# Delta rule rewritten: a shared inverse, a written order on three engines, output tiles as a stage of their own

## The chip, the cores and the metric

The kernel runs on one core of one Trainium2 chip. A core has five engines that run at the same time, each with its own queue that it works off in order: TensorE (PE; its weight loads appear as PEld), VectorE (DVE), ScalarE (ACT), GpSimd (POOL) and SyncE (SP, which here only issues DMA transfers). They wait for each other by semaphores. Matmuls read SBUF and write PSUM, which has 8 banks. The metric is the device time of one execution in microseconds (us).

## The reference

One step of a two-layer encoder over 2048 prompt tokens and 32 sample tokens (2080 rows of 1024), in float32. Layer A is a gated delta rule with 8 heads of 128; layer B is windowed attention.

```python
proj = x @ w_in                                   # q, k, v, z (1024 each), a, b
q, k, v = silu(short causal conv(proj)); q, k l2-normalised
beta = sigmoid(b);  g = -exp(a_log) * softplus(a + dt_bias);  gcum = cumsum(g) in a chunk
tmat = I + strict_lower(beta * k k^T * decay)     # decay = exp(gcum_i - gcum_j)
u, w = tmat^-1 (beta v),  tmat^-1 (beta k exp(gcum))
for chunk:                                        # S is a 128x128 state per head
    v_new = u - w S
    o = (q exp(gcum)) S + (q k^T * decay) v_new
    S = S exp(g_last) + (k exp(g_last - gcum))^T v_new
h = layer_norm(ALPHA * x + (rms_norm(o) * silu(z)) @ w_out)
y = layer_norm(ALPHA * h + attention(h))          # layer B: rotary q, shared k/v, sinks, gate
```

## The kernel before

**P1** (from 0 to about 700 us) projects the inputs, slab by slab of 128 columns over 5 token blocks of 416. Every product is made of three matmuls (high times high, high times low, low times high), so one block is 24 matmuls on PE (`project`). `P1.z` makes the gate z; blocks 0 to 2 come first, blocks 3 and 4 later, beside the delta rule. Results go to DRAM and come back by DMA.

**Delta** works through 17 chunks: 16 of 128 tokens and the 32 of the sample. Per chunk and in halves q of four heads: `decays` makes the decay matrix E (DVE and ACT), `lower` multiplies k k^T by it (tile npr), gathers the 32x32 diagonal blocks (nb) and lays them out with a DVE transpose (tile L, L414). `chain` inverts these blocks for all heads at once: 31 pairs of short instructions (L421 makes tm from L and Tt, L423 subtracts it from Tt), each waiting for the one before. It runs on GpSimd, for the second chunk alone on VectorE. `spread` turns the result Tt around (tcp, ucp) into t32 and u32; `invert` completes the 128x128 inverse u by five rounds of small matmuls (bps). `turn_k`, `turn_v`, `inside` make kd, vn and at, and fade k and q. `errors` (ks, rho, vp, vs) and `advance` (op, o, sp, Sp) are the recurrence over chunks; `scale` and `emit` normalise o, turn it (otr), multiply it by z and store it (s_g).

`run` is the loop. In iteration i chunk i is finished, chunk i+1 is inverted and chunk i+2 is begun. The order on PE is the order in which the code is written (`manual_schedule`); DVE, ACT and the DMA queues are ordered by a scheduler at build time.

**Filler**: between the steps `fill(us)` lets PE do other work of so many us: first z of blocks 3 and 4 (`P1.z`), then the output tiles **O1**. An output tile is 128 tokens: g is loaded (L727), split into high and low parts (g_hi on ACT L737, g_lo on GpSimd L738), multiplied by w_out in two halves of 24 matmuls (po, L751 to L753), added to x and normalised on DVE (L756 to L775), turned on PE (tr, L797) into hT and stored. g and hT share one buffer. After the last chunk the rest of the 17 tiles runs without the delta rule, with two gate blocks of P2 among them.

**P2** and **Attention** follow: the projections of layer B (PE bound) and the attention.

Of the kernel before, what the change touches and what calls it, by code (L numbers as in the profile page):

```python
# [43 lines left out]
def split_weights(nc, pool, src, sub):  # L44

    raw = pool.tile([128, KC, 128], F32, tag="w_raw", name="w_raw", bufs=1)
    hi = pool.tile([128, KC, 128], F32R, tag="w_hi", name="w_hi")
    lo = pool.tile([128, KC, 128], F32R, tag="w_lo", name="w_lo")
    nc.sync.dma_start(raw[:], src)
    nc.scalar.copy(hi[:], raw[:])  # L50
    sub.tensor_tensor(out=lo[:], in0=raw[:], in1=hi[:], op=ALU.subtract)  # L51
    return hi, lo

# [34 lines left out]
class P1:  # L88
# [3 lines left out]
    def __init__(self, tc, left, right, I, O, T, G):  # L92
# [4 lines left out]
        self.ppl = new_pool(tc, left, "p1_psl", 3, PSUM, side="left")  # L97
# [3 lines left out]
        self.ppr = new_pool(tc, right, "p1_psr", 3, PSUM, side="right")  # L101
# [32 lines left out]
    def ps(self):  # L134
        self.turn += 1
        return (self.ppl, self.ppr)[self.turn % 2].tile([128, 512], F32, tag="ps", name="ps")
# [75 lines left out]
    def z(self, blocks, pool, tags, ps, sub):  # L212
        nc = self.nc
        for h in range(8):
            w = split_weights(nc, self.wp, self.I["w_in"][24 + h], sub)
            for b in blocks:
# [7 lines left out]
                nc.sync.dma_start(self.T["z"][h, :, b * TB:(b + 1) * TB], z[:])  # L224

# [84 lines left out]
def rsqrt_newton(nc, pool, x, n, w, tag):  # L310
    V = nc.vector
    y = pool.tile([128, w], F32, tag=tag + "_y", name=tag + "_y")
# [3 lines left out]
    V.tensor_scalar(out=y[:n].bitcast(I32), in0=y[:n].bitcast(I32), scalar1=-1, scalar2=0x5F3759DF,  # L316
                    op0=ALU.mult, op1=ALU.add)
    for _ in range(3):
        V.scalar_tensor_tensor(out=t[:n], in0=x[:n], scalar=-0.5, in1=y[:n], op0=ALU.mult, op1=ALU.mult)
        V.tensor_tensor(out=t[:n], in0=t[:n], in1=y[:n], op=ALU.mult)  # L320
        V.scalar_tensor_tensor(out=y[:n], in0=t[:n], scalar=1.5, in1=y[:n], op0=ALU.add, op1=ALU.mult)
    return y
# [7 lines left out]
class Delta:  # L330


    def __init__(self, tc, es, I, O, T, G):
# [9 lines left out]
        self.pc = new_pool(tc, es, "d_pc", 2, PSUM, side=R)  # L343
        self.nm = one.tile([128, 128], F32, tag="nm", name="nm")
        nc.scalar.dma_start(self.nm[:], I["nm"])
        self.tinit = one.tile([128, 32, 8], F32, tag="tinit", name="tinit")
        nc.scalar.dma_start(self.tinit[:], I["tinit"])
        self.f = {}
        for k in ("t32", "u32", "m1"):
            self.f[k] = one.tile([128, 8, 64], F32, tag=k, name=k)  # L350
            nc.vector.memset(self.f[k][:], 0.0)
        self.u = one.tile([128, 8, 128], F32, tag="u", name="u")
        nc.vector.memset(self.u[:], 0.0)
        self.S = one.tile([128, 8, 128], F32, tag="Sp", name="Sp")
        nc.vector.memset(self.S[:], 0.0)
# [5 lines left out]
    def load(self, ch, name):  # L361
        nc, T, n = self.nc, self.T, ch.n
        ts = slice(ch.t0, ch.t0 + n)
        pool, bufs = (self.sml, 2) if name == "v" else (self.four, 4)
        tiles = []
        for q in range(2):
            hs = slice(q * 4, q * 4 + 4)
            t = pool.tile([128, 4, 128], F32, tag=name, name=name, bufs=bufs)
# [5 lines left out]
        setattr(ch, name, tiles)  # L374

    def decays(self, ch):
        nc, V, G = self.nc, self.nc.vector, self.G
        n, ti = ch.n, ch.ti
        ch.E = []
        for q in range(2):  # L380
# [3 lines left out]
            for j in range(4):  # L384
                nc.scalar.activation(E[:n, j, :n], E[:n, j, :n], AF.Exp, bias=G["ngc"][:n, ti, q * 4 + j:q * 4 + j + 1])
            V.tensor_tensor(out=E[:n, :, :n], in0=E[:n, :, :n], in1=self.bc(G["cc"][:n, ti, q * 4:q * 4 + 4], n, n),
                            op=ALU.mult)
            ch.E.append(E)

    def lower(self, ch):  # L390
# [4 lines left out]
        ch.nb = nb = self.sml.tile([128, 8, 32], F32, tag="nb", name="nb")  # L395
        for q in range(2):
# [5 lines left out]
            if q == 1:  # L402
                for b in range(n // 32):
                    bs = slice(32 * b, 32 * b + 32)
                    nc.scalar.copy(nb[bs], ch.npr[bs, :, bs])
            yield "kk"

    def chain(self, ch, P):

        nc, V = self.nc, self.nc.vector  # L410
        n = ch.n
        sml = self.sml
        L = sml.tile([128, 32, 32], F32, tag="L", name="L")
        V.transpose(L[:n], ch.nb[:n].rearrange("q p i -> q i p").unsqueeze(2).to_broadcast([n, 32, 4, 8]))  # L414
        Tt = self.two.tile([128, 32, 8], F32, tag="Tt", name="Tt")
        tm = sml.tile([128, 32, 8], F32, tag="tm", name="tm")
        nc.scalar.copy(Tt[:n], self.tinit[:n])
        for j in range(31):
            i0, w = j + 1, j // 4 + 1
            sh = [n, 31 - j, w]  # L420
            P.tensor_tensor(out=tm[:n, i0:, :w], in0=L[:n, i0:, j:j + 1].to_broadcast(sh),  # L421
                            in1=Tt[:n, j:j + 1, :w].to_broadcast(sh), op=ALU.mult)
            P.tensor_tensor(out=Tt[:n, i0:, :w], in0=Tt[:n, i0:, :w], in1=tm[:n, i0:, :w], op=ALU.subtract)  # L423
        ch.Tt = Tt

    def turn_k(self, ch):
        nc, G, n = self.nc, self.G, ch.n
        ch.kd = []
        for q in range(2):
# [8 lines left out]
            yield "tr"  # L438

    def turn_v(self, ch):  # L440
        nc, G, n = self.nc, self.G, ch.n
        ch.vn = []
        for q in range(2):
# [7 lines left out]
            yield "vtr"  # L451

    def inside(self, ch, by):
# [3 lines left out]
        for q in range(2):  # L457
# [11 lines left out]
            yield "gq"  # L469

    def spread(self, ch):
# [3 lines left out]
        u = self.u  # L475
        sml = self.sml
        tcp = sml.tile([128, 8, 8, 4], F32, tag="tcp", name="tcp")
        ucp = sml.tile([128, 8, 32], F32, tag="y1", name="ucp")
        V.transpose(tcp[:n].rearrange("q p c d -> q c d p"), ch.Tt[:n].rearrange("q i c -> q c i"))
        tcf = tcp[:].rearrange("q p c d -> q p (c d)")  # L480
        V.transpose(ucp[:n], tcf[:n])
        if n == 32:
            V.tensor_copy(u[:32, :, :32], ucp[:32])
            return
        t32, u32, m1, npr = self.f["t32"], self.f["u32"], self.f["m1"], ch.npr
        nc.scalar.copy(m1[0:32, :, 32:64], npr[0:32, :, 32:64])
        nc.scalar.copy(m1[64:96, :, 32:64], npr[64:96, :, 96:128])
        for b in range(4):
            bs = slice(32 * b, 32 * b + 32)
            cs = slice(32 * (b % 2), 32 * (b % 2) + 32)  # L490
            nc.scalar.copy(t32[bs, :, cs], tcf[bs])
            nc.scalar.copy(u32[bs, :, cs], ucp[bs])

    def invert(self, ch):
# [17 lines left out]
        yield "y1p"  # L512
# [6 lines left out]
        yield "up"  # L519
# [5 lines left out]
        yield "tp"  # L525
# [4 lines left out]
        yield "y2p"  # L530
# [4 lines left out]
        yield "u2p"  # L535

    def errors(self, ch):

        nc, V, n = self.nc, self.nc.vector, ch.n
        rho, ch.vs = [], []  # L540
        for q in range(2):
# [3 lines left out]
            rho.append(self.two.tile([128, 4, 128], F32, tag="rho", name="rho"))  # L545
            V.tensor_tensor(out=rho[q][:n], in0=ch.vn[q][:n], in1=ks[:n], op=ALU.subtract)
            yield "ks"
        for q in range(2):
            vp = self.pc.tile([128, 4, 128], F32, tag="sc", name="vp")
            for j in range(4):  # L550
                nc.tensor.matmul(vp[:n, j, :], self.u[:n, q * 4 + j, :n], rho[q][:n, j, :], start=True, stop=True)
            vs = self.two.tile([128, 4, 128], F32, tag="vs", name="vs", bufs=3)
            nc.scalar.copy(vs[:n], vp[:n])
            ch.vs.append(vs)
            yield "vp"

    def advance(self, ch):

        nc, V, G, S, n = self.nc, self.nc.vector, self.G, self.S, ch.n
        ch.o = []  # L560
        ch.X = X = self.sml.tile([128, 8], F32, tag="Xo", name="Xo", bufs=2)
        for q in range(2):
            op = self.pc.tile([128, 4, 128], F32, tag="sc", name="op")
            for j in range(4):
                h = q * 4 + j
# [830 lines left out]
```

## Time and profile before

| | us |
|---|---|
| three runs, median (lowest to highest) | 2401.82 (2398.37 to 2402.85) |
| the profiled execution | 2404.43 |
| its span, first to last instruction | 2402.4 |

Busy in that span, with each engine's share of it and its instructions:

```profile
PE 2228.8 (93%) x13778; PEld 2029.5 (84%) x13778; DVE 1392.3 (58%) x2648; ACT 898.5 (37%) x2197; POOL 929.5 (39%) x1413
```

And PE and the clock granted to it in 40 slices of 60 us, in tenths:

```profile
PE   7999999999989968888878897999999998999997
PEclk9999999999999979999898998999999999999998
```

A row of a group gives source line, engine, operation, "tile written<-tiles read", shapes and count, then the busy time in us, the mean of one in ns, and how long the engine stood idle before them and for whom. "Busy" of PE is modelled: neighbouring matmuls overlap, so a PE that is called busy can still be slower than its issue rate. The delta rule lies in slices 11 to 25, where the digits of PE fall.

### The profile page before, as it was taken

What the parts mean: (1) busy time and instruction counts of PE and PEld (TensorE: products, weight loads), DVE (VectorE), ACT (ScalarE), POOL (GpSimd) and SP (SyncE); (2) the same over time, 40 slices, a digit from 0 to 9 for tenths busy, and PEclk for the clock granted to TensorE, in tenths of its full rate; (3) what the DMA queues carried; (4) which work ended last, traced back from release to release, by engine and by line L of the source; (5) the groups of instructions that cost most, each with busy time, mean ns of one, the idle gap of its engine ahead of it and who ended that gap; (6) DMA issues with size and microseconds to landing.
All of it is one profiled execution on the core that took longest, in us unless ns stands there. A gap on an engine that the chain in (4) does not pass through costs nothing. (4 is left out here: it accounts for less than half of the span.)

```text
span 2402.4 us, 36689 instructions
## 1 busy us (share of the span) xinstructions
PE 2228.8 (93%) x13778; PEld 2029.5 (84%) x13778; DVE 1392.3 (58%) x2648; ACT 898.5 (37%) x2197; POOL 929.5 (39%) x1413
## 2 busy tenths in 40 slices
PE   7999999999989968888878897999999998999997
PEld 5999999999988857777777785899999986788885
DVE  3676666544437667777766766413444225667874
ACT  3344444333224454545444432221111235444451
POOL 1422212111203356565766644103433134555663
PEclk9999999999999979999898998999999999999998
DMA  5111211121236374555454446422222266233221
GB/s 181 62 73 67 76 71 63 71 80 67 100 105 139 94 189 83 134 119 118 120 129 102 123 125 191 146 80 101 68 74 75 75 154 178 80 97 106 88 67 57
DMA packets 268593, 247.79 MB, mean 103 GB/s; under 512 B 67600, under 2 KB 243792, under 8 KB 265072
## 3 DMA queue, kind: packets, MB, share of 16 engines
q1 hardware_dynamic: 259168, 233.50, 34.1%
q10 hardware_dynamic: 9248, 11.96, 1.6%
q8 instruction: 108, 1.77, 0.3%
q14 instruction: 69, 0.57, 0.1%
HBM read 154.57 MB, written 91.20 MB: 102 GB/s over the span
## 5 line engine op out<-in xcount | busy, mean ns | idle before, releaser
L69 PE MATMUL ps<-act_hi,w_hi 128*128 128x416 f32 x2000 | 708.6, 355 | 2.7 <-ACT w_hi L50 2.0
L71 PE MATMUL ps<-act_hi,w_lo 128*128 128x416 f32 x2000 | 702.6, 352 | 0.0
L70 PE MATMUL ps<-act_lo,w_hi 128*128 128x416 f32 x2000 | 701.9, 351 | 0.2 <-DVE act_lo L61 0.2
L69 PEld LDWEIGHTS ps<-act_hi,w_hi 128*128 128x128 f32 x2000 | 376.2, 188 | 8.6 <-ACT w_hi L50 2.3
L70 PEld LDWEIGHTS ps<-act_lo,w_hi 128*128 128x128 f32 x2000 | 377.0, 189 | 4.6 <-DVE act_lo L61 0.6
L71 PEld LDWEIGHTS ps<-act_hi,w_lo 128*128 128x128 f32 x2000 | 376.1, 188 | 5.5
L51 POOL TENSOR_TENSOR w_lo<-w_raw,w_hi 128x1024 fp32r<-128x1024 f32 x54 | 143.7, 2661 | 609.5 <-ACT w_hi L50 557.9
L421 POOL TENSOR_TENSOR tm<-L,Tt 128x60 f32<-128x60 f32 (+26 forms) x496 | 184.9, 373 | 261.4 <-DVE L L414 194.6
L180 DVE SCALAR_TENSOR_TENSOR y<-R,convw,y 128x2083 f32<-128x2083 f32 x72 | 171.6, 2384 | 121.1 <-ACT y L178 119.8
L423 POOL TENSOR_TENSOR Tt<-Tt,tm 128x60 f32<-128x60 f32 (+26 forms) x496 | 195.0, 393 | 38.5
L1140 POOL TENSOR_TENSOR P<-P,sm 128x384 f32<-128x384 f32 (+2 forms) x128 | 103.5, 830 | 159.3 <-DVE sm L1017 85.1
L210 ACT COPY R<-ps 128x416 f32<-128x416 f32 (+1 forms) x144 | 61.4, 449 | 208.4 <-PE ps L71 184.2
L1013 ACT ACTIVATE P<-S,nm 128x192 f32<-128x192 f32 (+2 forms) x260 | 104.7, 420 | 90.9 <-DVE nm L1006 43.7
L50 ACT CAST w_hi<-w_raw 128x1024 fp32r<-128x1024 f32 x62 | 65.0, 1049 | 193.5 <-PE ps L70 154.8
L880 POOL TENSOR_TENSOR rs<-rs,sin 128x416 f32<-128x416 f32 x50 | 71.3, 1426 | 147.4 <-DVE rs L879 103.0
L751 PE MATMUL po<-wo_hi,g_hi 128*128 128x512 f32 (+1 forms) x272 | 120.1, 441 | 0.0
L753 PE MATMUL po<-wo_hi,g_lo 128*128 128x512 f32 (+1 forms) x272 | 109.5, 402 | 0.0
L752 PE MATMUL po<-wo_lo,g_hi 128*128 128x512 f32 (+1 forms) x272 | 109.3, 402 | 0.0
L1153 PE MATMUL ot<-pt,vd 128*128 128x256 f32 x372 | 98.8, 392 | 3.5 <-DVE graw L1156 1.6
L1038 PE MATMUL po<-wo_hi,g_hi 128*128 128x512 f32 x240 | 100.0, 417 | 1.3 <-ACT wo_hi L700 1.3
L1039 PE MATMUL po<-wo_lo,g_hi 128*128 128x512 f32 x240 | 96.9, 404 | 2.1 <-DVE wo_lo L701 2.1
L566 PE MATMUL op<-Sp,q 128*128 128x128 f32 (+1 forms) x272 | 61.6, 313 | 37.4 <-ACT o L570 30.8
(263 smaller groups left out, 4187.1 us busy)
## 6 DMA issues: line engine op xcount, KB each, us to landing
w_raw<-in_w_in SPq DMA_DIRECT2D x40, 512.0 KB
w_raw<-in_b_w_in SPq DMA_DIRECT2D x20, 512.0 KB
s_z<-z SPq DMA_DIRECT2D x40, 208.0 KB
s_bz<-za SPq DMA_DIRECT2D x40, 208.0 KB
s_bq<-ra SPq DMA_DIRECT2D x40, 208.0 KB
s_q<-y SPq DMA_DIRECT2D x8, 1024.0 KB
s_k<-y SPq DMA_DIRECT2D x8, 1024.0 KB
s_v<-y SPq DMA_DIRECT2D x8, 1024.0 KB
```

The costliest lines, as they stand in the source:

```text
L51: sub.tensor_tensor(out=lo[:], in0=raw[:], in1=hi[:], op=ALU.subtract)
L69: nc.tensor.matmul(ps, hi[:, k, :], xh[:, k, :], start=(k == 0), stop=False)
L70: nc.tensor.matmul(ps, hi[:, k, :], xl[:, k, :], start=False, stop=False)
L71: nc.tensor.matmul(ps, lo[:, k, :], xh[:, k, :], start=False, stop=(k == KC - 1))
L180: nc.vector.scalar_tensor_tensor(out=y[:], in0=R[:, j:j + W], scalar=self.convw[:, i, j:j + 1], in1=y[:], op0=ALU.mult, op1=ALU.add)
L421: P.tensor_tensor(out=tm[:n, i0:, :w], in0=L[:n, i0:, j:j + 1].to_broadcast(sh), in1=Tt[:n, j:j + 1, :w].to_broadcast(sh), op=ALU.mult)
L423: P.tensor_tensor(out=Tt[:n, i0:, :w], in0=Tt[:n, i0:, :w], in1=tm[:n, i0:, :w], op=ALU.subtract)
L751: nc.tensor.matmul(ps[:n], ghi[:, k, :n], w[0][:, k, cs], start=(k == 0), stop=False)
L752: nc.tensor.matmul(ps[:n], ghi[:, k, :n], w[1][:, k, cs], start=False, stop=False)
L753: nc.tensor.matmul(ps[:n], glo[:, k, :n], w[0][:, k, cs], start=False, stop=(k == KC - 1))
L1013: nc.scalar.activation(P[u], src, AF.Exp, bias=nm[:, u:u + 1], scale=1.0, accum_out=sm[:, u:u + 1])
L1140: nc.gpsimd.tensor_tensor(out=P[:, u, :nj], in0=P[:, u, :nj], in1=f.unsqueeze(1).unsqueeze(3).to_broadcast([128, nj, 2, 64]), op=ALU.mult)
```

## The change

1. **The inverse is shared.** `chain` takes a range of the 31 steps. GpSimd does the first 24 (`SPLIT`), 48 instructions; VectorE does the last 7, 14 instructions, an iteration later. The first chunk's chain runs whole on VectorE, the second chunk's is shared.
2. **The order is written.** `manual_schedule` now holds for PE, DVE and ACT, and all steps are generators that `run` strings together one instruction or a few at a time. A chunk's end (`emit`) moves into the next iteration.
3. **The filler is split.** `first` (z of blocks 3 and 4) fills iterations 0 to 6, with 0.6 of the listed amounts. From iteration 7 to 14 nothing fills. `second` (the output tiles) starts where no new chunk is left (iteration 15) and the rest of it runs as a stage after the loop. Half the weights of w_out are split by `side()` at the end of iterations.
4. **The output tile.** g_lo is made on DVE instead of GpSimd, one step earlier (j == 3). After the loop hT has a buffer of its own (`o1_hT`), and the turning uses P2's PSUM banks. P2's first loads and weight slabs move into tile 8, its first gate block stays ahead of the last tile.
5. **Smaller ones.** v and z share two buffers (tag "vz"); t32 and u32 are written by four ACT instructions with a 0/1 scale instead of eight copies of 32 partitions; memsets move from DVE to GpSimd; the query-state product q S gets a PSUM bank of its own and is issued apart from the rest of op; P1's banks are divided 2 and 4 instead of 3 and 3; z's weights are fetched a slab ahead.

The inverse on DVE. Rows as the program holds them, one chunk in the middle of the loop; tm and Tt are the chain's tiles, L its transposed blocks, z the emission, npr the lower product, Sp the state. Before:

```order
L546 TENSOR_TENSOR rho<-vn,ks 128x512 x2
L386 TENSOR_TENSOR E<-E,t_cc 128x512
L479 STREAM_TRANSPOSE tcp<-Tt 128x32x8
L481 STREAM_TRANSPOSE ucp<-tcp 128x256
L401 TENSOR_TENSOR npr<-g,E 128x512
L577 SCALAR_TENSOR_TENSOR Sp<-Sp,t_egl,sp 128x128 x4
L401 TENSOR_TENSOR npr<-g,E 128x512
L414 STREAM_TRANSPOSE L<-nb 128x1024
```

The same place of the loop now:

```order
L680 TENSOR_TENSOR z<-otr,z 128x512
L442 TENSOR_TENSOR npr<-g,E 128x512 x2
L516 TENSOR_TENSOR k<-k,gb 128x512 x2
L462 TENSOR_TENSOR tm<-L,Tt 128x7x7
L465 TENSOR_TENSOR Tt<-Tt,tm 128x7x7
L462 TENSOR_TENSOR tm<-L,Tt 128x6x7
L465 TENSOR_TENSOR Tt<-Tt,tm 128x6x7
L680 TENSOR_TENSOR z<-otr,z 128x512
L462 TENSOR_TENSOR tm<-L,Tt 128x5x7
L465 TENSOR_TENSOR Tt<-Tt,tm 128x5x7
L451 STREAM_TRANSPOSE L<-nb 128x1024
```

Before, the finished chain (tcp reads Tt) stands ahead of npr and L, from which the next chain starts. Now only three of DVE's own pairs (for the chunk ahead) stand between the end of GpSimd's part and the L of the next one; tcp comes some twenty rows later.

PE around the state update, in the middle of the loop. Before, with po, the output tile's product, between the steps (g is k k^T of the chunk after next, sp the state's addition):

```order
L400 MATMUL g<-k 128x128 x4
L574 MATMUL sp<-vs,kd 128x128 x4
L751 MATMUL po<-wo_hi,g_hi 128x512
L752 MATMUL po<-wo_lo,g_hi 128x512
L753 MATMUL po<-wo_hi,g_lo 128x512
L751 MATMUL po<-wo_hi,g_hi 128x512
L752 MATMUL po<-wo_lo,g_hi 128x512
L753 MATMUL po<-wo_hi,g_lo 128x512
L400 MATMUL g<-k 128x128 x4
```

And now:

```order
L619 MATMUL op<-vs,at 128x128 x4
L633 MATMUL sp<-vs,kd 128x128 x8
L615 MATMUL op<-Sp,q 128x128 x4
L619 MATMUL op<-vs,at 128x128 x4
L590 MATMUL ks<-Sp,k 128x128 x4
L489 MATMUL vtr<-ident,v 128x128 x4
L590 MATMUL ks<-Sp,k 128x128 x4
```

The output tile's rows are gone from the loop and stand behind it. On the DMA queue the tiles' transfers now repeat in this order, where g is a load for the tile after next and r (the rows of x) one for the next:

```order
L853 DMA g<-s_g 128x8x128
L950 DMA s_h<-r 128x1024
L855 DMA r<-in_x 128x1024
L929 DMA s_hT<-hT 128x8x128
L853 DMA g<-s_g 128x8x128
```

The diff, cut to its core:

```diff
+    SPLIT = 24
...
-    def chain(self, ch, P):
+    def chain(self, ch, P, a, z):
...
-        for j in range(31):
+        for j in range(a, z):
             i0, w = j + 1, j // 4 + 1
...
-            by.tensor_tensor(out=kt[:, :, :n], in0=kt[:, :, :n], in1=eg, op=ALU.mult)
-            by.tensor_tensor(out=qt[:, :, :n], in0=qt[:, :, :n], in1=eg, op=ALU.mult)
+    def fade(self, ch):
+        n = ch.n
+        for x in (ch.k, ch.q):
+            for q in range(2):
+                self.nc.vector.tensor_tensor(out=x[q][:, :, :n], in0=x[q][:, :, :n], in1=ch.gb[q][:, :, :n], op=ALU.mult)
+                yield
...
+        for dst, src in ((t32, tcf), (u32, ucp)):
+            for c in range(2):
+                nc.scalar.activation(dst[:, :, 32 * c:32 * c + 32], src[:], AF.Copy, scale=self.sides[:, c:c + 1])
...
+            more = 0.6 if i < 7 else 0.0 if n2 else 1.0
+            if not n2:
+                fill = second.give
+            vp, a, sq, t = (gen(f, c) for f, c in ((self.changes, ch), (self.advance, ch), (self.squares, ch),
+                                                   (lambda c: self.chain(c, V, self.SPLIT, 31), nx)))
+            low = gen(self.lower, n2)
+            go(z, low, low)
...
+            go(vp, vp, x, x, t, t, t, t, low, z, t, t, low)
+            if n2:
+                drain(self.chain(n2, P, 0, self.SPLIT))
...
+            go(e, t, t)
+            drain(t)
+            if nx:
+                self.spread(nx)
+            go(w, e, x, x)
...
+            go(v, r, r, r, g, r, r, r, v, d, r, d, r)
+            self.load(ch, "z")
...
+            z, x = self.emit(ch), gen(self.fade, n2)
...
-        nc.gpsimd.tensor_tensor(out=glo[:, :, :n], in0=g[:, :, :n], in1=ghi[:, :, :n], op=ALU.subtract)
+        nc.vector.tensor_tensor(out=glo[:, :, :n], in0=g[:, :, :n], in1=ghi[:, :, :n], op=ALU.subtract)
...
-    with tc.manual_schedule(engines={mybir.EngineType.PE}):
-        delta.run(chunks, filler.give, done)
-        right.close()
-        p2 = P2(tc, right, I, O, T)
-        p2.slab(0, nc.gpsimd)
-        p2.slab(1, nc.gpsimd)
-        filler.rest()
+    with tc.manual_schedule(engines={ET.PE, ET.DVE, ET.Activation}):
+        delta.run(chunks, first, second, side, done)
+    right.close()
+    hp = new_pool(tc, right, "o1_hT", 1, side="right")
+    o1[0].room = lambda: hp.tile([128, KC, 128], F32, tag="hT", name="hT")
+    p2.append(P2(tc, right, I, O, T))
+    o1[0].bank = p2[0].ps
+    with tc.manual_schedule(engines={ET.PE}):
+        second.rest()
```

More of the change, by code (lines that the diff above doesn't have):

```diff
@@ L602, in emit @@
+            yield
     def emit(self, ch):
@@ new lines, in run @@
+            go(t, t)
+            if nx and nx.n > 32:
+                self.corners(nx)
+            if last:
+                done(last)
+            fill(2 * more)
+            go(seen, a, t, t)
+            fill(more)
+            go(sq, seen)
+            if n2:
+                self.load(n2, "q", (1,))
+                self.load(n2, "v", (1,))
+            go(a, t, seen, sq)
+            fill(2 * more)
+            if not ch:
+                break
+            if i + 2 == len(chunks):
+                self.between(ch)
```

439 lines of the change are left out of this document (259 added, 180 removed).

## The prediction

> **What bounds the kernel now.** I read the busy time by stretches first, to find the stage in which no engine is full; then the waits in it; then the timeline of the engine that is waited for.
>
> ```profile
> 600.00:700.00 100.00, 100.00 (x535) 99.16 (x534) 41.16 (x51) 20.89 (x32) 15.53 (x6) 1.00 0.29 97
> ...
> 1100.00:1200.00 100.00, 84.56 (x730) 74.58 (x729) 76.93 (x174) 44.41 (x129) 67.25 (x162) 0.91 0.51 116
> ...
> 1600.00:1700.00 100.00, 100.00 (x604) 98.75 (x602) 32.34 (x64) 14.45 (x28) 29.76 (x19) 1.00 0.24 83
> ```
>
> The columns after the length are PE, PEld, DVE, ACT, POOL, then clock, DMA share and GB/s. In the projections before and behind (first and last row) PE is full at clock 1.00; the change leaves their matmuls as they are, and I count them at nothing: PE covers the moved memsets, banks and fetches there, and would show any that it does not cover as a gap. In the delta rule (second row) nobody is full. Its period:
>
> ```profile
> L544 PE MATMUL ks<-Sp,k x272: 270/275/583, 798.4 to 1432.9; 128*128 128x128 f32 x128, 128*32 128x128 f32 x8
> ```
>
> From the first ks to the last chunk's there are 16 periods: (1432.9 - 798.4) / 16 = 39.7 us a chunk. Who is waited for between 1000 and 1400 us, the two longest rows of the waits:
>
> ```profile
> POOL tm L421 <- DVE L L414: 52.4, 6, 13.5
> DVE tcp L479 <- POOL Tt L423: 51.6, 9, 7.3
> ```
>
> GpSimd waits for L, and DVE waits for GpSimd's result: a ring. One turn of it on GpSimd:
>
> ```profile
> 1018.45 0.26 POOL L421 TENSOR_TENSOR tm<-L,Tt 128x31 f32<-128x31 f32 x1 [4.00 <-DVE Xo L594]
> ...
> 1040.44 0.63 POOL L423 TENSOR_TENSOR Tt<-Tt,tm 128x48 f32<-128x48 f32 x1
> ...
> 1045.71 0.20 POOL L423 TENSOR_TENSOR Tt<-Tt,tm 128x8 f32<-128x8 f32 x1
> ...
> 1060.15 0.25 POOL L421 TENSOR_TENSOR tm<-L,Tt 128x31 f32<-128x31 f32 x1 [2.62 <-DVE Xo L594]
> ```
>
> The 62 instructions take 27.5 us (1018.45 to 1045.91); then 14.2 us pass until the next chain starts, of which 2.4 are g_lo of an output tile. In them tcp, npr, nb and L follow each other on DVE and ACT, between output tile work. 27.5 + 14.2 = 41.7, one period. So the ring sets the time here, not PE.
>
> **The change, part by part.**
>
> *The ring.* The same timeline gives GpSimd's new part: the 48th instruction ends at 1041.07, so 22.6 us. What closes the new ring is short, as the order rows show: GpSimd's end, four chain instructions, z, two chain instructions, L, GpSimd's start. Their durations on DVE, from the second chunk's chain, which runs there already, and from the first L:
>
> ```profile
> 779.38 0.24 DVE L421 TENSOR_TENSOR tm<-L,Tt 128x76 f32<-128x76 f32 x1
> 779.66 0.24 DVE L423 TENSOR_TENSOR Tt<-Tt,tm 128x76 f32<-128x76 f32 x1
> ...
> 727.24 2.07 DVE L414 STREAM_TRANSPOSE L<-nb 128x1024 f32<-128x1024 f32 x1
> ```
>
> Dependent chain instructions start 0.26 us apart: 6 x 0.26 = 1.6, z 0.6 (its mean is that of other 512-wide reads of PSUM, 0.68 for L756 below, less the overlap), L 2.0, hand-overs 0.3. Ring: 22.6 + 4.5 = **27.1 us**. The new wait is that of the first of the four for GpSimd; behind it on DVE stand z, L, the state update and all else of the chunk, so a late GpSimd delays everything.
>
> *DVE's load.* A chunk's stretch, and four groups of the output tile:
>
> ```profile
> 1116.00:1156.00 40.00, 33.91 (x296) 29.94 (x295) 30.25 (x69) 19.69 (x58) 24.90 (x61) 0.93 0.65 136
> ...
> L773 DVE SCALAR_TENSOR_TENSOR r<-r,mv,ln_g 128x512 f32<-128x512 f32 (+1 forms) x34 | 28.1, 859 | 0.0
> L775 DVE SCALAR_TENSOR_TENSOR r<-r,ln_y,ln_b 128x512 f32<-128x512 f32 (+1 forms) x34 | 24.5, 760 | 0.4
> L756 DVE SCALAR_TENSOR_TENSOR r<-r,po 128x512 f32<-128x512 f32 (+1 forms) x34 | 23.2, 682 | 25.2 <-PE po L753 24.6 <-DMA r<-in_x 0.5
> L757 DVE BATCH_NORM_STATS2 st<-r 128x6 f32<-128x512 f32 (+1 forms) x34 | 23.3, 685 | 0.4
> ```
>
> The four groups are 99.1 / 17 = 5.8 us a tile; with hT's copy and a dozen small steps about 9. Of 30.25 us of DVE some 21 are then the delta rule's. Add 14 chain instructions, 14 x 0.26 = 3.6: 24.9 us, below the ring. Fading, norms and E keep their counts. A written order makes DVE wait where a scheduler could step aside; I add 1 us: **28 us a chunk** from iteration 7 on, between 25 (load alone) and 32 (ring and 5 us of such waits).
>
> *PE's load.* Eight matmuls of the chunk's kind start 0.89 us before the next group:
>
> ```profile
> 1130.82 1.05 PE L400 MATMUL g<-k 128*128 128x128 f32 x8
> 1131.71 0.39 PE L566 MATMUL op<-Sp,q 128*128 128x128 f32 x2
> ...
> 1136.73 0.39 PE L752 MATMUL po<-wo_lo,g_hi 128*128 128x512 f32 x1
> 1136.96 0.40 PE L753 MATMUL po<-wo_hi,g_lo 128*128 128x512 f32 x1
> ...
> 1139.73 1.15 PE L516 MATMUL bps<-u,y 64*64 64x64 f32 x32 [1.23 <-ACT y L511]
> ```
>
> Seven steps have 16 such instructions a chunk (ks is x272 for 17 chunks above) and three turnings 8: 136 x 0.111 = 15.1; the five bps rounds 1.1 each: 20.7 us. Below the ring too. In iterations 0 to 6 the z filler adds 11 x 0.6 = 6.6 us of PE, which fits beside, and a block and a half of z on DVE (about 2.5 us with the weights' split), which does not: 30.5 us a chunk.
>
> *Before the loop.* Now the first chunk's chain takes DVE, and the second one's goes to GpSimd beside the first inversion:
>
> ```profile
> 760.19 0.68 DVE L479 STREAM_TRANSPOSE tcp<-Tt 128x256 f32<-128x256 f32 x1
> ...
> 798.50 0.19 DVE L423 TENSOR_TENSOR Tt<-Tt,tm 128x28 f32<-128x28 f32 x1
> ```
>
> The first L comes at 727 in either; 62 x 0.26 = 16 us of chain on DVE, with 12 us of other steps laid between, end near 757 instead of 760. From tcp to the first ks DVE spent 38 us, in which 50 instructions of the second chain lay before and among the inversion; without them 20 are left (five rounds at 2 us, their copies, E, the z filler). The loop starts near **777** instead of 798.4; I keep 770 and 790 as ends.
>
> *The output stage.* What the loop no longer covers: 48 matmuls 0.23 apart are 11.1 us, 8 turnings 0.9: 12 us of PE a tile, with some slips 12.5. The last iterations have 27 us of it as filler, 2.3 tiles; 14.7 are left: 184, and the two gate blocks 9 (24 matmuls 0.188 apart each, 535 in 100 us above), and 8 for P2's loads, whose casts stand in ACT's queue before g_hi: 201 us. DVE has 9 + 1.4 (g_lo now) = 10.4 of each 12.5, so PE leads narrowly. r of the next tile waits for the last turning of the tile before; the stores of that tile and the load of g queue around it on SP.
>
> *The sum.* Two rows for it: a split of w_out's rows, and the copy of the last turned tile before.
>
> ```profile
> L701 DVE TENSOR_TENSOR wo_lo<-wo_raw,wo_hi 128x1024 fp32r<-128x1024 f32 x8 | 9.9, 1236 | 5.8 <-ACT wo_hi L700 5.8
> ...
> 1532.20 0.27 ACT L799 COPY hT<-tr 128x128 f32<-128x128 f32 x1 [4.29 <-issue]
> ```
>
> 777 + 7 x 30.5 + 8 x 28 + 9 (eight of w_out's splits at 1.24 us of DVE are 9.9, less a little that hides) + 58 (iterations 15 to 17 without a new chunk, about 19 each) + 201 = 1482.5. Against 1532.5 that is 50 us less. The profiled execution (2404.4) lies 2.6 over the median of the three runs, so the forecast is 2401.8 - 50 = **2352**.
>
> **Rivals.**
>
> *The clock falls.* PE is now less filled than in any stretch of before but one:
>
> ```profile
> PE otr L609 <- DVE o L600: 8.0, 1, 8.0
> ...
> 837.00:877.00 40.00, 22.87 (x210) 20.64 (x208) 25.86 (x47) 23.27 (x57) 25.49 (x55) 0.74 0.72 206
> ```
>
> There, between 837 and 877 us, with 210 matmuls and one pause of 8.0 us for DVE, the granted clock was 0.74, against 1.00 where PE is full. Eight iterations now have no filler at all. At 0.74 PE needs 20.7 / 0.74 = 28 us, and about 4 us a chunk in which it must wait for DVE and ACT in turn: 32, over 15 chunks +60 us: 2412, slower. It decides from 31.3 us a chunk, a clock of 0.76. Against it: that stretch has the pause of 8 us, and my walk through the new order finds none over 2 us. The Trainium skill, TensorE: Matmul & The Clock Gate (What's actually happening), says that the clock halves after an idle window of about 3.4 us and returns after as long a busy one; the trace's 1.00 in filled stretches agrees, and by the rule pauses under 2 us would leave the clock up.
>
> *The output tiles stay slow.* The second half of each tile, behind the loop, before:
>
> ```profile
> 1462.46 0.69 DVE L756 SCALAR_TENSOR_TENSOR r<-r,po 128x512 f32<-128x512 f32 x1 [1.68 <-PE po L753]
> ...
> 1521.99 0.68 DVE L756 SCALAR_TENSOR_TENSOR r<-r,po 32x512 f32<-32x512 f32 x1 [4.61 <-PE po L753]
> ...
> 1491.33 1.11 PE L797 MATMUL tr<-ident,r 128*128 128x128 f32 x4 [9.76 <-ACT hT L799]
> ...
> 1487.13 1.04 ACT L737 CAST g_hi<-g 128x1024 fp32r<-128x1024 f32 x1 [11.71 <-DMA g<-s_g]
> ```
>
> Three tiles in 59.5 us, two gate blocks (9) among them: 16.8 each, not 12.5. If that stays, 14.7 x 4.3 = +63: 2415, slower. For it: the transfers per tile are the same. Against it: g and hT shared a buffer there, so that g waited for hT's store; now they don't, and g is asked for two tiles ahead.
>
> *GpSimd and DVE hinder each other more.*
>
> ```profile
> 1116.36 0.34 POOL L421 TENSOR_TENSOR tm<-L,Tt 128x75 f32<-128x75 f32 x1
> 1116.78 0.69 POOL L423 TENSOR_TENSOR Tt<-Tt,tm 128x75 f32<-128x75 f32 x1
> ```
>
> Of two equal-sized instructions one took 0.35 us longer; DVE was fading k just then. If a denser DVE adds 8 such hits, the ring is 2.8 longer where its slack of 0.9 ends: +1.9 x 15 = 28: 2380. The Trainium skill, SBUF — State Buffer (SBUF: two separate sides), has GpSimd and a DVE operation with two SBUF inputs exclude each other for a whole instruction; the trace agrees. By that rule the most would be DVE's ten such wide operations a chunk. Against it: the 22.6 us were measured with as many, those of the output tile included.
>
> *DVE's load is all that counts* (25 a chunk, 28 with z, loop from 770, tiles of 12): 50 + 15 x 2.9 + 7 + 7 = 108 us saved, 2294.
>
> **How the numbers follow.** Forecast 0.55 (on its own 2330 to 2375), more hindrance 0.15 (2380), load alone 0.10 (2294), clock 0.10 (2412), slow tiles 0.10 (2415). A measurement of this kernel can tell about 0.2% from no change. Faster: the first three, 0.80; the last two are slower, 0.16, but for 0.04 where they come out half. The range takes in the forecast, the hindrance and most of both ends: 2302 to 2414.
>
> **What would show it.** First ks near 777 and then every 30.5, later 28 us; GpSimd's 48 instructions in 22 to 25 us with 3 to 5 us of idle time between chains; the largest wait in the loop DVE's tm for GpSimd's Tt, or GpSimd's for L; clock over 0.9 in the loop; behind it about 15 tiles 12 to 13 us apart at clock 1.00. The forecast is wrong if chunks take over 31.3 us, or if tiles take over 15.9 us (50 / 14.7 more).

## The result, and the profile after

| | before | changed |
|---|---|---|
| median, us (lowest to highest) | 2400.62 (2398.37 to 2402.85) | 2457.09 (2455.64 to 2461.63) |
| span of the profiled execution | 2402.4 | 2459.8 |

The changed kernel takes 1.0238 times as long (95% interval 1.0221 to 1.0256): 56 us slower, where 50 us less was forecast. From the page of the changed kernel, busy time by engine, and PE and its granted clock in 40 slices of 61.5 us:

```profile
PE 2251.2 (92%) x13778; PEld 2052.3 (83%) x13778; DVE 1441.0 (59%) x2883; ACT 875.9 (36%) x2133; POOL 781.3 (32%) x1184
...
PE   8999999999988888687777899999999998999997
...
PEclk9999999999988888888888999999999999999999
```

PE's matmuls are as many as before. The clock lies at 8 tenths in slices 12 to 22, the loop and its beginning, and at 9 in all others. The same from the busy time by stretches (columns as in the prediction) in the loop and in the output stage behind it:

```profile
1100.00:1200.00 100.00, 72.42 (x701) 67.07 (x701) 72.08 (x174) 50.10 (x143) 45.66 (x130) 0.83 0.48 110
...
1500.00:1600.00 100.00, 99.62 (x491) 81.99 (x490) 66.70 (x176) 16.87 (x26) 2.42 (x1) 1.00 0.49 150
```

In the first of these rows, in the loop, every engine is idle for a quarter of the time or more. GpSimd, the engine that should have set the pace, is busy for 46%. Where the steps begin, from the timelines of PE and ACT: the first ks at all, those of iterations 7 and 15, the first matmul of the first output tile behind the loop, and the copy of the last turned tile:

```profile
771.46 2.05 PE L590 MATMUL ks<-Sp,k 128*128 128x128 f32 x16
...
1018.72 1.16 PE L590 MATMUL ks<-Sp,k 128*128 128x128 f32 x8 [0.28 <-DVE Sp L638]
...
1298.60 1.16 PE L590 MATMUL ks<-Sp,k 128*128 128x128 f32 x8
...
1381.28 0.80 PE L877 MATMUL po<-wo_hi,g_hi 128*128 128x512 f32 x1 [0.78 <-DVE hT L928]
...
1591.37 0.27 ACT L926 COPY hT<-ps 128x128 f32<-128x128 f32 x1
```

The loop did get shorter. (1298.6 - 771.5) / 15 = 35.1 us a chunk; iteration 15 began 103 us earlier. Its ks before:

```profile
1401.89 1.95 PE L544 MATMUL ks<-Sp,k 128*128 128x128 f32 x16
```

Counted to the same chunk, the period before was (1401.9 - 798.4) / 15 = 40.2 us; the 39.7 of the prediction takes in the short last one.

But from that point on the stages now take 292.8 us instead of 1532.2 - 1401.9 = 130.3. Of these 162 us more, 139 are twelve more output tiles behind the delta rule (15 instead of 3), and 24 are its last iterations, which grew from 58.9 to 82.7. 162 us given back for 103 won is 59 us, the loss (57 by the spans of the two profiled executions). The tiles cost about 12 us each behind the loop, as was forecast. So the main question is why a loop relieved of them still takes 35 us a chunk.

The waits between the first ks and that of iteration 15 (sum, times, longest) answer it:

```profile
POOL tm L462 <- DVE tm L462: 207.6, 13, 24.5
...
PE bps L575 <- DVE ta L571: 83.3, 14, 14.2
DVE E L417 <- DMA gb<-s_gcum: 74.6, 25, 11.5
```

GpSimd waits for DVE, PE waits for DVE's ta (a tile that one round of the inversion hands to the next), and DVE waits for a transfer: gb, the sums of the decay that E is made from. Over the whole run, the addition that makes E, before (L382) and now (L417), with the idle time of DVE just ahead of it in the last column:

```profile
L382 DVE TENSOR_TENSOR E<-gb,nm 128x512 f32<-128x512 f32 (+1 forms) x34 | 24.3, 716 | 9.1 <-DMA gb<-s_gcum 9.1
```

```profile
L417 DVE TENSOR_TENSOR E<-gb,nm 128x512 f32<-128x512 f32 (+1 forms) x34 | 23.4, 690 | 85.7 <-DMA gb<-s_gcum 85.5
```

9.1 us have become 85.5. The 9.1 are all the first chunk's, ahead of the loop:

```profile
716.78 0.69 DVE L382 TENSOR_TENSOR E<-gb,nm 128x512 f32<-128x512 f32 x1 [7.71 <-DMA gb<-s_gcum]
718.87 0.69 DVE L382 TENSOR_TENSOR E<-gb,nm 128x512 f32<-128x512 f32 x1 [1.40 <-DMA gb<-s_gcum]
```

Now the first chunk has 11.0 of the 85.5. The rest is in the loop, where there was no such wait before. One iteration shows how it comes about. On DVE:

```profile
1100.89 1.44 DVE L516 TENSOR_TENSOR q<-q,gb 128x512 f32<-128x512 f32 x2
...
1104.63 1.38 DVE L565 TENSOR_TENSOR u<-u,bps 64x512 f32<-64x512 f32 x2
1109.81 0.69 DVE L417 TENSOR_TENSOR E<-gb,nm 128x512 f32<-128x512 f32 x1 [3.80 <-DMA gb<-s_gcum]
...
1112.64 0.69 DVE L417 TENSOR_TENSOR E<-gb,nm 128x512 f32<-128x512 f32 x1 [1.92 <-DMA gb<-s_gcum]
...
1114.18 0.67 DVE L571 TENSOR_TENSOR ta<-t,bps 64x512 f32<-64x512 f32 x1
```

On the queue of transfers (SP), and on PE:

```profile
1096.92 0.46 SPq L407 DMA_DIRECT2D q<-s_q  x1
1097.47 0.46 SPq L407 DMA_DIRECT2D k<-s_k  x1
1098.03 0.45 SPq L407 DMA_DIRECT2D z<-s_z  x1
1098.75 0.36 SPq L407 DMA_DIRECT2D k<-s_k  x1
1101.59 1.12 SPq L405 DMA_DIRECT2D gb<-s_gcum  x2
```

```profile
1106.15 1.11 PE L569 MATMUL bps<-y,u 64*64 64x64 f32 x16 [1.34 <-DVE u L565]
1107.19 1.16 PE L615 MATMUL op<-Sp,q 128*128 128x128 f32 x8
1114.90 1.97 PE L575 MATMUL bps<-ta,npr 64*64 64x64 f32 x16 [6.55 <-DVE ta L571]
...
1117.84 1.97 PE L580 MATMUL bps<-u,ta 64*64 64x64 f32 x16
...
1120.64 2.91 PE L441 MATMUL g<-k 128*128 128x128 f32 x16
1123.39 1.95 PE L601 MATMUL vp<-vn,u 128*128 128x128 f32 x16
```

In iteration i, gb of chunk i+3 is loaded into the buffers of gb of chunk i+1 (there are four, two halves of two chunks), so its load waits until q of chunk i+1 is faded (the first row on DVE). It is asked for at 1101.59, behind four other loads, and its two halves land 8 and 11 us later. In DVE's written order both additions stand ahead of ta, and ta needs nothing of them. PE then has no work for 6.55 us, of which DVE's two waits for gb are 3.80 + 1.92. The two rounds of bps behind that pause run at little over half their pace (1.97 us against 1.11 for L569, the round before it); the low clock of the loop comes with such stretches.

Before, a load of gb was asked for a whole chunk ahead of its addition. Counted in order, the addition at 1111.11 reads what was asked for at 1068.80, 42 us earlier:

```profile
1068.80 0.36 SPq L370 DMA_DIRECT2D gb<-s_gcum  x1
```

```profile
1111.11 0.68 DVE L382 TENSOR_TENSOR E<-gb,nm 128x512 f32<-128x512 f32 x1
```

For the chunks from the fourth on, 35 to 61 us lay between the two; now 8 to 14 do (5 and 6 for the short last chunk). It is not the written order alone that closed this distance. By the two programs two more parts of the change did, in as many buffers as before: `fade` now treats chunk i+1 in iteration i, where `inside` used to fade chunk i+2, so buffers come free an iteration later; and `decays` is begun for chunk i+3, where it was chunk i+2, an iteration earlier. No run puts either back as it was, or gives gb more buffers.

### The profile page after: what moved, and what is told of

It is laid out like the page before. It is cut to its first block, busy times and chain, and to the rows that moved or that the text cites. A ratio compares the mean times of both kernels' runs of the same rounds, so it can differ in the third digit from the quotient of the medians.

```text
span 2459.8 us, 36690 instructions
## 1 busy us (share of the span) xinstructions
PE 2251.2 (92%) x13778; PEld 2052.3 (83%) x13778; DVE 1441.0 (59%) x2883; ACT 875.9 (36%) x2133; POOL 781.3 (32%) x1184
## 4 chain that ended last, share of the span: by engine, by line
PE 72%; DMA 10%; DVE 10%; ACT 3%; issue 2%; POOL 1%; SPq 0%; DVEq 0%; ACTq 0%; POOLq 0%
PE ps L77 15%; PE ps L79 15%; PE ps L78 14%; DMA gb<-s_gcum 5%; PE ot L1286 3%; PE po L1171 2%; PE po L1172 2%; PE po L1173 2%; PE S L1265 2%; PE po L877 2%; PE po L879 2%; PE po L878 2%; DMA act_raw<-s_hT 1%; PE tr L1280 1%; PE g L441 1%
## 5 line engine op out<-in xcount | busy, mean ns | idle before, releaser
L462 POOL TENSOR_TENSOR tm<-L,Tt 128x60 f32<-128x60 f32 (+21 forms) x384 | 125.4, 327 | 325.9 <-DVE tm L462 207.6
L465 POOL TENSOR_TENSOR Tt<-Tt,tm 128x60 f32<-128x60 f32 (+21 forms) x384 | 140.3, 365 | 30.1
L218 ACT COPY R<-ps 128x416 f32<-128x416 f32 (+1 forms) x144 | 61.5, 450 | 209.4 <-PE ps L79 184.3
L877 PE MATMUL po<-wo_hi,g_hi 128*128 128x512 f32 (+1 forms) x272 | 113.5, 417 | 2.0 <-ACT g_hi L863 1.2
L575 PE MATMUL bps<-ta,npr 64*64 64x64 f32 x256 | 29.0, 297 | 83.3 <-DVE ta L571 83.3
```

The lines of the kernel that those rows point to most:

```text
L877: nc.tensor.matmul(ps[:n], ghi[:, k, :n], w[0][:, k, cs], start=(k == 0), stop=False)
```

## The experiments

All edits are of the changed kernel except b1, which is of the kernel before. The steps of each run, read from its profiled execution as above (chunk: mean from ks to ks; rest: from the ks of iteration 15 to the last copy of hT), and the median of all its executions:

| run | first ks | chunk, iterations 0 to 6 | chunk, 7 to 14 | ks of 15 | rest | median time |
|---|---|---|---|---|---|---|
| forecast | 777 | 30.5 | 29.1 | 1223.5 | 259 | 2352 |
| changed kernel | 771.5 | 35.3 | 35.0 | 1298.6 | 292.8 | 2457.1 |
| e1 | 770.9 | 30.1 | 33.0 | 1245.8 | 285.8 | 2405.8 |
| e2 | 770.6 | 30.1 | 30.7 | 1226.9 | 291.2 | 2390.2 |
| e3 | 770.5 | 34.5 | 34.0 | 1284.3 | 280.5 | 2440.1 |
| e4 | 770.8 | 35.3 | 40.2 | 1339.3 | 249.7 | 2461.3 |
| f1 | 773.8 | 29.0 | 30.3 | 1218.8 | 287.1 | 2373.3 |
| f2 | 770.2 | 33.7 | 35.6 | 1291.5 | 298.8 | 2462.2 |
| f3 | 772.8 | 30.5 | 32.9 | 1249.0 | 270.3 | 2382.6 |
| f4 | 772.1 | 30.0 | 31.2 | 1231.7 | 286.7 | 2393.9 |
| g1 | 769.0 | 29.0 | 32.4 | 1231.0 | 268.1 | 2369.3 |
| g2 | 771.9 | 28.5 | 32.3 | 1229.7 | 264.8 | 2368.7 |
| h1 | 770.2 | 29.1 | 33.0 | 1238.2 | 267.3 | 2376.1 |

(The forecast's 29.1 is its 28 with the 9 us of w_out's splits spread over eight iterations.)

**e1: the buffers of gb come free earlier.**

```diff
-            go(vp, vp, x, x, t, t, t, t, low, z, t, t, low)
+            go(vp, vp, x, x, x, x)
+            if n3:
+                self.load(n3, "gb")
+            go(t, t, t, t, low, z, t, t, low)
...
-            if n3:
-                self.load(n3, "gb")
             go(t, t)
...
-            go(w, e, x, x)
+            go(w, e)
```

> Edit: q is faded right behind k, so that the buffers of gb come free, and the loads of the next gb stand, some 8 us earlier in each iteration; nothing else moves. Theory G (DVE, in its written order, waits for gb: 85.5 us in 27 waits, and the inversion's ta and PE behind it): the waits for gb fall below 20 us in sum, the stretch from ks to ks goes from 34.5 to about 30 us where nothing fills, first ks of chunk 15 from 1298.6 to about 1235, total 2385 to 2400. Theory C (low clock, 0.80 to 0.86, and the load of DVE set the loop; the wait for gb only fills what is spare): the same time goes to other waits, a stretch stays over 33 us, total 2440 to 2457. The cost of the edit itself under both: 1.4 us of DVE move ahead of the chain, which GpSimd's idle 13 us a chunk covers.

51 us less than the changed kernel (1.0021 of before, 1.0009 to 1.0033). The first line is the addition of E over the run; the second a wait of PE between 1000 and 1200 us:

```profile
L417 DVE TENSOR_TENSOR E<-gb,nm 128x512 f32<-128x512 f32 (+1 forms) x34 | 23.3, 687 | 11.1 <-DMA gb<-s_gcum 10.6
```

```profile
PE gq L504 <- DMA q<-s_q: 29.2, 6, 6.5
```

The wait for gb fell from 85.5 to 10.6, which are the first chunk's again, as theory G has it: 17 to 21 us now lie between load and addition (15 for the last chunk). Iterations 0 to 6 lie at 30.1. Later 33.0 are left, and another transfer has taken gb's place: PE now waits for the second half of q, 4.9 us a time here (2.0 before 980 us). That load stands in SP's queue behind one of v, and v waits for a store:

```profile
SPq L407 <- DMA s_g<-z: 73.7, 12, 9.9
```

v and z share two buffers since the change, so v's load waits until the emitted z of the chunk before is stored, and every load behind it in the queue waits too.

**e2: E stands later on DVE.**

```diff
-            go(v, r, r, r, g, r, r, r, v, d, r, d, r)
+            go(v, r, r, r, g, r, r, r, v, r, r)
...
-            go(k, w, v, seen, d, v, k)
+            go(k, w, v, seen, v, k)
...
-            go(d, d, o)
+            go(d, d, d, o)
...
-            go(v, o)
+            go(v, o, d, d)
```

> Edit: gb is loaded when it was, but on DVE the two additions of E (and what follows them, exponentials on ACT and the product with beta) stand behind the inversion's ta and the emission's norms. Theory G: what costs is not E itself but what is queued behind the waiting addition: PE's wait for ta (83 us in 14 between 800 and 1400) goes, a stretch falls to 30 to 31 us, total 2385 to 2410. Theory C: over 33 us, total 2440 to 2457. In between (2415 to 2440) if E then comes late for npr, which starts the next inverse, and the wait reappears there.

67 us less than the changed kernel, and half a per cent faster than before: 0.9949 (0.9935 to 0.9964). The load is where it was; only what stands behind it on DVE differs. The waits between the first ks and that of iteration 15, and PE's round that needs ta (its idle time before it in the last column):

```profile
DVE E L417 <- DMA gb<-s_gcum: 24.8, 19, 5.6
```

```profile
L575 PE MATMUL bps<-ta,npr 64*64 64x64 f32 x256 | 23.2, 256 | 0.7 <-DVE ta L571 0.7
```

PE's wait for ta went from 83.3 us to 0.7, and the chunks to 30.1 and 30.7 us. Iteration 15 begins at 1226.9, where the forecast had 1223.5. Theory G holds; theory C, by which the clock and DVE's load would have kept the loop over 33 us, falls.

**e3: GpSimd does all pairs** (`SPLIT = 31`, nothing else).

> Edit: GpSimd does all 31 pairs (SPLIT = 31), DVE none but the first chunk's. The prediction's theory (the ring of GpSimd's chain and L sets the period): the ring is 4.4 us longer and the time 15 x 4.4 = 66 us longer, 2520. Theory G (the ring has slack now, GpSimd waits 192 us in 12 of the chunks for DVE): within 15 us of 2457, to either side, since the chain's end still comes before DVE asks for it, and DVE has 3.6 us a chunk less to do.

17 us less than the changed kernel, just beyond what G allowed and against the sign of the ring. The ring, 4.4 us longer here, was not what set the changed loop.

**e4: output tiles as filler from iteration 11.**

```diff
-            more = 0.6 if i < 7 else 0.0 if n2 else 1.0
-            if not n2:
+            more = 0.6 if i < 7 else 0.0 if i < 11 else 1.0
+            if i >= 11:
                 fill = second.give
```

> Edit: from iteration 11 on (not 15) the output tiles fill the pauses of the loop, in the full listed amounts, about 11 us of PE and one tile an iteration. If a stretch of 34.5 us has room for it (PE 20.7 + 11, DVE 25 + 9 of 34.5, with the wait for gb as cover), 4 tiles leave the stage behind the loop: 4 x 12 = 48 us less, minus the loop's growth: 2415 to 2430. If DVE's written order makes each added wait show (g_hi in ACT's queue, g_lo and r in DVE's), the four iterations grow by 9 to 12 us each and the time stays within 10 us of 2457.

4 us more than the changed kernel, within the intervals of the two. Iteration 15 begins 40.7 us later and the rest is 43.1 us shorter, a trade at par. The pauses of this written order were no room: a tile that was put there cost about what it costs behind the loop.

**f1 and f2: the split, without the wait for gb** (e2 with `SPLIT = 31`, and with `SPLIT = 16`).

> Edit: e2_decay_late, and GpSimd does all 31 pairs. There the loop takes 30.7 us a chunk, DVE is busy 84% of it (209.8 of 250 us) and GpSimd waits for DVE about 8 us a chunk. If DVE's load sets the loop now: 14 instructions of 0.26 us fewer are 3.6 us a chunk, of which GpSimd's 4.4 us longer part gives little back: 2390 - 15 x 2 to 3 = 2345 to 2365. If the ring sets it, as predicted (27.1 + 4.4 = 31.5): 15 x 1 to 4 us longer, 2400 to 2450. No change (2385 to 2395) if the pauses between hand-overs set it and both have room.

> Edit: e2_decay_late, and GpSimd does 16 pairs, DVE 15: 16 more instructions on DVE a chunk, 4.2 us. DVE's load sets the loop: 15 x 4.2 = 63 us longer, 2450. The ring sets it: GpSimd's part is about 8 us shorter, DVE's 4.2 longer, so 2335 to 2390.

f1 takes 17 us less than e2 (0.9888 of before, 0.9872 to 0.9904), f2 72 us more. GpSimd's first instruction of a chain, with its idle time before it, in e2 (24 pairs), f1 (31) and f2 (16):

```profile
1081.92 0.26 POOL L462 TENSOR_TENSOR tm<-L,Tt 128x31 f32<-128x31 f32 x1 [11.18 <-DVE Tt L465]
```

```profile
1042.12 0.26 POOL L462 TENSOR_TENSOR tm<-L,Tt 128x31 f32<-128x31 f32 x1 [1.41 <-DVE L L451]
```

```profile
1119.16 0.31 POOL L462 TENSOR_TENSOR tm<-L,Tt 128x31 f32<-128x31 f32 x1 [25.45 <-DVE tm L462]
```

With fewer pairs GpSimd only waits longer for DVE. With 31 its chain (26 to 28 us in f1, from its timeline) and a pause, 0.8 to 2.7 us in ten of fifteen chunks, make up the period: GpSimd is nearly full there. By this sum its chain sets the loop of f1, at 30.3 us and not at the 31.5 that the expectation had for the ring. For f2 there is a second cause beside DVE's load: the 16 added instructions stand in one block ahead of tcp, and PE waited for what follows from it in five iterations between 1000 and 1200 us, 6.2 us a time, where the loop is 4.9 us a chunk longer than in e2:

```profile
PE bps L556 <- ACT t L539: 31.2, 5, 6.3
```

**f3: no filler behind iteration 6** (e2 with `more = 0.6 if i < 7 else 0.0`).

> Edit: e2_decay_late, and nothing fills the last iterations; all 17 output tiles are made behind the loop. From the ks of chunk 15 to the first tile behind the loop there are 82.8 us now, with two tiles in them. If filler is free there, as the prediction had it: two more tiles at 11.8 behind the loop, 2390 + 24 = 2414. If it lies in front of the recurrence on PE and adds to it: the last iterations lose about what the stage gains, 2380 to 2396.

8 us less than e2 by the medians, but the ratios to before do not tell the two apart (0.9931, 0.9903 to 0.9958, and 0.9949, 0.9935 to 0.9964), and its profiled execution is its slowest, 2391.7. Nor is it the run that was meant: po's high matmuls, between 1000 and 1320 us of it, are

```profile
L877 PE MATMUL po<-wo_hi,g_hi x48: 388/394/775, 1015.2 to 1318.6; 128*128 128x512 f32 x48
```

16 of these make a tile: the scheduler laid three tiles of the second block of written order among the matmuls of the first, some of them as early as 1015. The question whether filler is free in the last iterations has no run of its own; rows below bear on it.

**f4: P2's loads in tile 12** (e2 with `if i == 12` for the loads).

> Edit: e2_decay_late, and the loads for the next projections stand in tile 12 of the output stage, not in tile 8. Now two of its tiles last 16.8 and 17.4 us instead of 11.8: there the copy of hT stands behind the casts of these loads in ACT's queue, and the next turning on PE waits 6.1 and 4.6 us. If the casts wait for their transfers wherever they stand: 2390 again, within 4. If it was the stores of the tiles before that made them late: up to 10 less, 2380 to 2385. Later loads may also leave the first gate block without its data: up to 2400.

Within 4 us of e2, as it was expected if the casts wait for their transfers wherever they stand. The pauses of PE ahead of a turning in the stage, from start to start, went from 6.1 and 4.6 us to 4.2 and 2.1, but nothing came of it in the time. In e2 these rows of ACT show such a tile: the copy of hT stands behind casts that wait 12.24 us for their load.

```profile
1360.74 1.68 ACT L68 CAST act_hi<-act_raw 128x832 fp32r<-128x832 f32 x2 [12.24 <-DMA act_raw<-s_hT]
1362.32 0.58 ACT L926 COPY hT<-ps 128x512 f32<-128x512 f32 x1
```

**b1: one part of the change alone, in the kernel before.**

```diff
         for j in range(31):
+            P = P if j < 24 else V
             i0, w = j + 1, j // 4 + 1
```

> Edit: the kernel before, with one part of the change alone: in the chain of every chunk the last 7 pairs are issued on DVE (the scheduler places them). The prediction's theory of the time before (the ring of GpSimd's chain, tcp, L sets 39.7 us a chunk): GpSimd's 14 short instructions take 4.9 us, on DVE 14 x 0.26 = 3.6, so the ring is 1.3 us shorter and 15 x 1.3 = 20 us are won, 2380; with an extra hand-over and DVE's other work between them, 0 to 20, 2380 to 2402. If DVE's load and its in-order waits decide there too, as e3 and f1 showed for the new loop: 15 x 1 to 3.6 us longer, 2415 to 2455.

No change: 1.0000 (0.9990 to 1.0010). Between 1000 and 1400 us, before and in b1:

```profile
1000.00:1400.00 400.00, 338.92 (x2918) 300.80 (x2917) 284.73 (x674) 186.42 (x559) 251.71 (x616) 0.93 0.49 118
```

```profile
1000.00:1400.00 400.00, 342.47 (x2977) 301.06 (x2976) 309.85 (x825) 187.88 (x564) 210.82 (x480) 0.94 0.51 120
```

GpSimd is relieved of 41 us in ten chunks, DVE takes 25 more, and the loop does not move. That lies at the edge of what the ring allowed, and the loss that DVE's load alone would have given is not there either: what GpSimd gave up, DVE took, inside the same circle. To share the inverse is worth nothing by itself there, and in the new loop the runs that do not share it are 17 us faster (e3 and f1).

**g1, g2 and h1: put together.** g1 is f1 with f3's edit. g2 is f1 with half the listed amounts of output tiles from iteration 11 on. h1 is g2 with `SPLIT = 28`.

```diff
-            more = 0.6 if i < 7 else 0.0 if n2 else 1.0
-            if not n2:
+            more = 0.6 if i < 7 else 0.0 if i < 11 else 0.5 if n2 else 1.0
+            if i >= 11:
                 fill = second.give
```

> Edit: f1_late_split31 with the filler of f3_late_nofill: the written order has no output tile in the loop any more, and the scheduler may lay the matmuls of the stage behind into the pauses of the loop (in f3 it put some 138 of them, nearly three tiles, between 1015 and 1310 us). If the gains add, as they concern different places: 2373 - 8 = 2365, within 5. If DVE is what the spread tiles cost (9 us a tile), and f1 won just that: 2370 to 2380.

> Edit: f1_late_split31, and from iteration 11 on output tiles fill the loop with half the listed amounts (5.5 us of PE, half a tile, an iteration). DVE is idle for 18% of 30.3 us, 5.5 us, and half a tile needs 4.5 of it. If that idle time can be used: two tiles leave the stage, 2373 - 20 = 2353. If each instruction put into a written order adds its own time (e4: four tiles cost the loop what they saved behind it): 2365 to 2385.

> Edit: g2_split31_fill11 with SPLIT = 28. With 24 pairs on GpSimd (e2) its chain takes 20 to 22 us and it then waits 6 to 12 us for DVE: DVE sets the loop. With 31 (f1, g2) its chain takes 26 to 28 us and it waits 1.4 to 2.6 us: now the ring of GpSimd's chain sets it. Between them: 28 pairs take about 25 us on GpSimd and add 6 x 0.26 = 1.6 us to DVE. If the two limits cross there, a chunk takes 0.5 to 1 us less than with either: 2369 - 8 to 15 = 2354 to 2361. If DVE's instructions cost more than they relieve, as f2 showed (4.8 us a chunk for 16): 2369 to 2380.

g1 and g2 are the fastest, 2369.3 and 2368.7: 0.9876 (0.9861 to 0.9891) and 0.9875 (0.9858 to 0.9891) of before. Their intervals overlap with that of f1 (0.9888, 0.9872 to 0.9904), so neither edit shows a gain over it: f3's 8 us did not add, and the half tiles of g2 did not win the 20 us that free room would have given. h1 lies 7 us above g2 (0.9895, 0.9875 to 0.9915, again overlapping): no crossing of the two limits shows, and what a pair costs on DVE against GpSimd is not settled by it.

## Why the prediction was wrong

*The loop (438 us forecast from the first ks to that of iteration 15, 446.5 with the splits).* This step failed, at one place: "my walk through the new order finds none over 2 us". The forecast named one new wait on DVE, for GpSimd, and asked what stands behind it. It did not ask the same of the additions of E. "Fading, norms and E keep their counts" is true of the counts, but fading now comes an iteration later and E an iteration earlier, so that the load between them comes late, and the written order puts the additions ahead of ta. The sum allowed 1 us a chunk for waits of a written order; in the 15 chunks the wait for gb measured 74.6 us on DVE, 5.0 a chunk, and the wait for ta behind it 83.3 on PE. With E elsewhere (e2) the loop takes 456.3 us and its steps 30.1 and 30.7 us, near the 30.5 and 29.1 of the sum; so 72 of the 105 us between forecast and result (1298.6 - 1226.9) are what this wait held up. e1, another edit against the same wait, wins 53 of them (1298.6 - 1245.8).

*The ring and DVE's load.* The 24 pairs took mostly 20 to 22 us where 22.6 were forecast, and the ring did not close in any run with 24: GpSimd waited 13 to 17 us in most chunks of the changed kernel, and 6 to 12 in most of e2. "Below the ring" was the wrong way round: DVE and what it waits for set the loop, as f1 shows (f2 agrees, but has a second cause). Whether GpSimd's chain set the old loop stays open: b1 shortens it and wins nothing, but it gives DVE as much. That e2 comes near the sum all the same is in part luck: the ring and DVE's load were estimated within 3 us of each other, 27.1 and 24.9.

*Before the loop.* Right: the first ks at 771.5, forecast 777, with 770 as the lower end.

*The last iterations.* This term was mis-sized: 58 us forecast (no row shows its 19 an iteration), 82.7 measured (1298.6 to 1381.3), with 2 tiles in them instead of 2.3. The sum counted the tiles there as free. From the ks of chunk 15 to the end of the delta rule, before and now:

```profile
1401.89:1460.80 58.91, 58.91 (x347) 46.69 (x345) 38.81 (x127) 14.47 (x47) 15.60 (x30) 1.00 0.58 168
```

```profile
1298.60:1381.28 82.68, 62.36 (x435) 49.92 (x433) 48.77 (x147) 23.22 (x72) 19.45 (x47) 0.88 0.30 82
```

Before, PE was busy throughout, at clock 1.00 and with three tiles among its work. Now it has two tiles, pauses for 20.3 us and has a clock of 0.88. In e2, where the stretch is as long, these waits between 1230 and 1312 us stand in it (the new state for the sample, and the state update, which waits for a product that stands on PE behind 12 matmuls of an output tile, one of which waits 3.4 us itself, for g_lo):

```profile
PE ks L590 <- DMA Sp<-in_state_delta: 6.4, 1, 6.4
...
DVE Sp L638 <- PE sp L633: 7.9, 2, 7.3
```

By their place the tiles delay the recurrence in the written order. But three of them fitted into 58.9 us before, so the tiles alone are not the 25 us that the forecast lacks; by size the pauses of PE are most of them. No run takes the tiles away alone, and how the 25 us divide stays open.

*The output stage.* Right within 10 us: 201 forecast for 14.7 tiles and the rest, 210 measured for 15. Undisturbed tiles are 11.8 us apart at clock 1.00, not 16.8. That this comes of g and hT no longer sharing a buffer fits, but no run tests it.

*The sum.* 75 to the ks of iteration 15, 25 in the last iterations, 9 in the stage, 109 on the last copy of hT (1591.4 for 1482.5); the time is 105 over the forecast.

*The rivals.* None named the cause. "The clock falls" gave the right side, and its point was met (over 31.3 us a chunk), but as a consequence, with the clock above its 0.76: between 1000 and 1200 us it is 0.81 in the changed kernel and 0.89 in e2, where no edit touches PE's own work. What the prediction wrote of the Trainium skill's rule (TensorE: Matmul & The Clock Gate, What's actually happening) came about in its first half: the pause of 6.55 us, over the 3.4 of the rule, was followed by matmuls at half pace. The return took longer than the busy window of about 3.4 us that the prediction quotes: some 7 us of work in the iteration shown, and there the measurement decides. "Slow tiles" fell: 11.8 us a tile. Hindrance between GpSimd and DVE would have made the chain longer; it got shorter.

## What to carry to other kernels

Where an order is written by hand, list for every instruction that reads a transfer what stands behind it on its engine, and place it last among what can run without it: with the load asked for at the same place, the loop's waits for gb were 74.6 us and PE's behind them 83.3, and with its reader moved 24.8 and at most 0.7. Where steps move between iterations, count how far each load stands ahead of its reader: 35 to 61 us here before, 8 to 14 after. A load's lateness is set by the last reader of its buffer and by the queue it stands in, so moving one load forward may only make the next one late (gb, then q). Work that is moved out of a loop's pauses must be paid for behind it, so the loop has to shrink by that much: here twelve tiles were 139 us behind the loop, and the loop won 103.

## What was not expected of the hardware

A pause on PE cost more than itself. After the 6.55 us without work (rows of the result) PE ran at half pace from 1114.90 until about 1122: the round at 1117.84 still took 1.97 us for 1.11, and the sixteen matmuls at 1120.64 took 2.91 us, where those at 1123.39 took 1.95, their full pace. The granted clock of these ten us (0.50, the first number behind the busy times):

```profile
1112.50:1122.50 10.00, 7.60 (x49) 7.04 (x50) 7.60 (x17) 5.36 (x12) 2.12 (x6) 0.50 0.11 28
```

That is 7 us of work at half pace, by estimate 3.5 us on top of the pause. Of the 14 waits for ta in the loop 13 are 3.5 us or longer, so a price of this kind is paid in nearly every chunk.
